# Cleared rows by ScalarE, pair sums in the last stage, a guard around unused positions, and products that nobody reads

## Chip, cores and metric

The kernel runs on one core of a Trainium2 chip. The metric is the device time of one execution in microseconds (us); the time before is the median of three runs. Engines are named as in the profile: PE is TensorE (PEld its weight loads), DVE is VectorE, ACT is ScalarE, POOL is GpSimd, SP is SyncE, whose queue issues most transfers.

## What is computed

An encoder layer over 1024 tokens of 1024 channels: a mixer (neighbourhood attention, RWKV-7 in both directions, pooling), a residual with layer norm, and then a mixture of experts. The change touches only the second half. There each token picks one of 4 groups and in it the best 2 of 8 experts; each expert is a gated MLP of width 512; the two results are weighted and added, and a second residual with layer norm ends the layer:

```
gate = pg_sel[:, None] * jax.nn.softmax(top_l, axis=-1)      # 2 weights for each token
hb = jax.nn.silu(xb @ w_gate[e]) * (xb @ w_up[e])            # for each block of an expert's tokens
y  = (hb @ w_down[e]) * wt[:, None]
f  = segment_sum(y, token)                                   # two rows for each token
x  = layer_norm(ALPHA * x + g2 * f) * ln2_gain + ln2_bias
```

## The kernel before

**Three stages matter.** The router (`route`, `router`) sorts tokens to experts; its instructions are ordered by a scheduler. The expert stage and the last stage (both in `experts`, the last one planned in `tail_plan`) are written out engine by engine, with semaphores.

**Router.** For each of the 2 x 8 columns of token places, GpSimd makes a one-hot matrix (L1267) and ScalarE scales it with the row number plus one (L1268). TensorE multiplies these with block one-hots (L1323), which gives for each of at most 50 positions the 128 rows that belong to it: `idx[:, g]` for reading, `idx[:, 50 + g]` for writing. An unused slot gets a row number beyond the last row, and the transfer skips it. So the buffers `xg` that receive rows must have been cleared: GpSimd does it with one memset of 4096 columns (L1275), behind its last one-hot (`issue_after`). A number for each position says how it is worked: 0 unused, 1 for 32 tokens, 2 for 64, 3 for 128. VectorE forms all these numbers in a chain of small operations (L1230 to L1356).

**Expert stage.** A position is up to 128 tokens of one expert. `pipeline` runs for TensorE, ScalarE and VectorE, `step(g)`: load the count of position g+1, `head(g)` (gate and up products, L1713 for 128 tokens, L1721 for fewer), `rows(g+1)` (transposes of the next position's rows, L1692), `down(g-1)` (down products, L1747 and L1758), `turn(g)` (transposes of the hidden values, L1728), then `step(g+1)`. TensorE is thus always one position ahead with heads. `by_size` chooses one of three bodies by branches; with few tokens the products write to 32 or 64 columns of the array (128\*32, 128\*64 in the profile) and several share it. The first 16 positions are always used; from there on branches ask whether a position is used (`if_used`). Steps are nested, so after the last used position, 36 here, TensorE and VectorE enter 37 with count 0, skip its bodies, do `down(36)` and jump to the end. GpSimd's queue gathers rows of a position from HBM (`gather`, L1648, size chosen by branches), four positions ahead, and scatters results to `ys` in HBM (L1656), to row 2 x token + j for choice j. SyncE's queue loads expert weights into three buffers (L1577); weights of the first three positions are loaded in the router. Those of position g wait for the gate-up products of g-3.

**End of the expert stage.** SyncE (`finish`) loads gain and bias of the last norm into the first half of `xg` (`late`), the residual rows x1 (L1589), and once all scatters have landed the result rows of `ys` in eight transfers of 1 MB, `l0` to `l7` (L1595). In transfer tt partition p gets both rows of token 128 tt + p.

**Last stage.** For each of 8 tiles of 128 tokens: TensorE multiplies the two result rows with diagonal matrices of the gates (`dg`, built by ScalarE and VectorE, L1906 and L1907), 4 products 128\*128 by 512 columns; in tiles 2 and 5 two more products with `alpha` add the residual (L1866). Tile tt uses the pair of banks tt mod 3. Otherwise VectorE adds the residual while it sums (L1878); for tiles 2 and 5 ScalarE sums (L1875). Then mean (L1883, VectorE), squares and root (L1895, L1897, ScalarE), reciprocal and a product (L1887, L1888, VectorE), normalising (L1901, ScalarE), times gain and plus bias (L1891, L1892, VectorE), and the output transfer (L1639). Each engine works its list in order and waits by the lists' counts. [...]

## Time and profile before

| | us |
|---|---|
| median of three runs (1575.29 to 1577.81) | 1575.91 |
| the profiled execution | 1565.44 |
| its span, first to last instruction | 1563.6 |
| router's last part, until the expert stage opens | to 947.7 |
| expert stage | 947.7 to 1508.5 |
| last stage | 1508.5 to 1563.6 |

Over the span TensorE is busy 87%, VectorE 50%, ScalarE 37%, GpSimd 24%; the mean granted clock of TensorE is 0.924.

How to read the rows below. A timeline row has the start and the length in us, the engine, the line of the kernel, the operation, out<-in, shapes and the number of merged instructions; in brackets stands the idle time just before and what ended it ("issue": nothing that the profile shows). Product shapes are rows\*columns of the array, then the output. [...] A group row has the count, then busy us and mean ns of one, then idle time before.

### The profile page before, as it was taken

What the parts mean: (1) busy time and instruction counts of PE and PEld (TensorE: products, weight loads), DVE (VectorE), ACT (ScalarE), POOL (GpSimd) and SP (SyncE); (2) the same over time, 40 slices, a digit from 0 to 9 for tenths busy, and PEclk for the clock granted to TensorE, in tenths of its full rate; (3) what the DMA queues carried; (4) which work ended last, traced back from release to release, by engine and by line L of the source; (5) the groups of instructions that cost most, each with busy time, mean ns of one, the idle gap of its engine ahead of it and who ended that gap; (6) DMA issues with size and microseconds to landing.
All of it is one profiled execution on the core that took longest, in us unless ns stands there. A gap on an engine that the chain in (4) does not pass through costs nothing. (4 is left out here: it accounts for less than half of the span.)

```text
span 1563.6 us, 24661 instructions
## 1 busy us (share of the span) xinstructions
PE 1367.4 (87%) x8190; PEld 923.9 (59%) x8190; DVE 778.7 (50%) x2002; ACT 571.8 (37%) x1182; POOL 380.4 (24%) x442
## 2 busy tenths in 40 slices
PE   5989999988869899999899745999999999899856
PEld 5778778766546677677788643444444444444422
DVE  6775886855883566565667972111111121211117
ACT  5663433414575667676544430000001000100006
POOL 3331232351337313700403331011101101111000
PEclk8999999996868899989999857999999999999968
DMA  9868899866422325315564475898878987998764
GB/s 259 223 200 303 284 318 327 298 211 186 145 64 69 93 72 150 88 35 150 187 262 162 167 275 208 338 351 324 330 291 341 380 324 306 362 369 349 262 248 193
DMA packets 163373, 371.49 MB, mean 238 GB/s; under 512 B 22880, under 2 KB 99009, under 8 KB 154227
## 3 DMA queue, kind: packets, MB, share of 16 engines
q1 hardware_dynamic: 155555, 350.59, 63.2%
q0 software_dynamic: 7632, 18.51, 3.7%
q8 instruction: 106, 1.74, 0.4%
q14 instruction: 80, 0.66, 0.1%
HBM read 365.47 MB, written 65.44 MB: 276 GB/s over the span
## 5 line engine op out<-in xcount | busy, mean ns | idle before, releaser
L1713 PE MATMUL m_pgu<-w,m_xT 128*128 128x512 f32 x448 | 197.0, 598 | 7.4 <-issue 7.2
L1713 PEld LDWEIGHTS m_pgu<-w,m_xT 128*128 128x128 f32 x448 | 84.7, 192 | 110.4 <-issue 110.3
L1656 POOL DMA_INDIRECT ys_s<-m_y,m_idx x37 | 35.0, 946 | 467.4 <-DVE m_y L1786 266.5
L197 PE MATMUL pg<-ul,w_h 128*128 128x512 f32 x320 | 128.2, 401 | 0.2 <-DVE ul L295 0.2
L196 PE MATMUL pg<-uh,w_h 128*128 128x512 f32 x320 | 126.7, 402 | 1.4 <-ACT uh L294 0.7
L198 PE MATMUL pg<-uh,w_l 128*128 128x512 f32 x320 | 126.8, 396 | 0.0
L1721 PE MATMUL m_pgu<-w,m_xT 128*32 128x256 f32 (+1 forms) x1312 | 108.0, 420 | 8.7 <-issue 8.3
L1747 PE MATMUL m_py<-w,m_hT 128*128 128x512 f32 x224 | 98.7, 594 | 9.6 <-issue 9.6
L1825 DVE TENSOR_TENSOR m_h<-m_sil,m_pgu 128x512 f32<-128x512 f32 x14 | 9.6, 688 | 192.4 <-PE m_pgu L1713 192.4
L1721 PEld LDWEIGHTS m_pgu<-w,m_xT 128*32 128x32 f32 (+1 forms) x1312 | 53.6, 116 | 54.5 <-issue 34.2
L210 DVE SCALAR_TENSOR_TENSOR acc<-wm,sc_c,acc 128x256 f32<-128x256 f32 x112 | 62.3, 557 | 27.8 <-DMA wm<-in_w_mod_dram 18.9
L1747 PEld LDWEIGHTS m_py<-w,m_hT 128*128 128x128 f32 x224 | 41.5, 190 | 57.1 <-issue 57.1
L1828 DVE TENSOR_TENSOR m_h<-m_sil,m_pgu 64x256 f32<-64x256 f32 (+1 forms) x23 | 10.8, 471 | 121.0 <-ACT m_sil L1796 121.0
L196 PEld LDWEIGHTS pg<-uh,w_h 128*128 128x128 f32 x320 | 60.6, 191 | 15.3 <-ACT uh L294 1.6
L197 PEld LDWEIGHTS pg<-ul,w_h 128*128 128x128 f32 x320 | 61.0, 191 | 14.1 <-issue 0.7
L198 PEld LDWEIGHTS pg<-uh,w_l 128*128 128x128 f32 x320 | 61.1, 191 | 13.3 <-issue 0.7
L945 DVE SCALAR_TENSOR_TENSOR sn<-s,fc,sf 64x64 f32<-64x64 f32 x168 | 47.5, 283 | 41.7 <-PE s L936 38.6
L756 PE MATMUL g<-zi,bk 64*128 64x128 f32 x384 | 54.2, 320 | 15.2 <-DMA bk<-bkd 9.3
L1758 PE MATMUL m_py<-w,m_hT 128*32 128x256 f32 (+1 forms) x656 | 56.6, 418 | 12.2 <-issue 12.2
L1781 DVE TENSOR_TENSOR m_y<-m_py,m_g 128x512 f32<-128x512 f32 x28 | 19.4, 692 | 88.0 <-PE m_py L1747 88.0
L756 PEld LDWEIGHTS g<-zi,bk 64*128 64x128 f32 x384 | 46.6, 219 | 28.0 <-issue 10.6
L1786 DVE TENSOR_TENSOR m_y<-m_py,m_g 32x256 f32<-32x256 f32 (+1 forms) x82 | 37.0, 451 | 52.3 <-PE m_py L1758 51.1
(523 smaller groups left out, 3017.8 us busy)
## 6 DMA issues: line engine op xcount, KB each, us to landing
w<-in_moe_w_gate_dram SPq DMA_DIRECT2D x37, 2048.0 KB, 8.4
w<-in_moe_w_up_dram SPq DMA_DIRECT2D x37, 2048.0 KB, 12.9
w<-in_moe_w_down_dram SPq DMA_DIRECT2D x37, 2048.0 KB, 15.9
wm<-in_w_mod_dram SPq DMA_DIRECT2D x128, 128.0 KB, 4.6
w<-in_w_in_dram SPq DMA_DIRECT2D x21, 512.0 KB, 6.7
hd<-h SPq DMA_DIRECT2D x18, 512.0 KB, 4.5
wm<-in_w_mod_dram SPq DMA_DIRECT2D x16, 512.0 KB, 6.3
w<-ys_s SPq DMA_DIRECT2D x8, 1024.0 KB, 13.0
```

Source lines behind the costliest of these rows:

```text
L196: mm(out, lh[0], rh[0], start=start, stop=False)
L197: mm(out, lh[0], rh[1], start=False, stop=False)
L198: mm(out, lh[1], rh[0], start=False, stop=stop)
L210: nc.vector.scalar_tensor_tensor(acc, wm, self.sc_c[:, k:k + 1], acc, op0=OP.mult, op1=OP.add)
L756: nc.tensor.matmul(pa[h][:, j], bk[hs, j], zr[hs, j], start=True, stop=True)
L945: nc.vector.scalar_tensor_tensor(sn[H[h], H[h]], p[H[h], 2, H[h]], fc[H[h]], sf[H[h], H[h]], op0=OP.mult, op1=OP.add)
L1656: e.indirect_dma_start(out=self.ys_d, out_offset=off(idx[0:t, NP + g:NP + g + 1]), in_=y[0:t, g % NY], in_offset=None, bounds_check=2 * S ...
L1713: i = mm(pgu[q], xT[:, k], w[:, k], start=k == 0, stop=k == 7)
L1721: i = mm(pgu[0][o:o + t, 0:n], xT[:, k, 0:t], w[:, k, c:c + n], start=k == 0, stop=k == 7)
L1747: i = mm(py[nh], hT[:, 128 * f:128 * f + 128], wd[b][:, f, 512 * nh:512 * nh + 512], start=f == 0, stop=f == 3)
L1758: i = mm(py[0][o:o + t, 0:n], hT[:, 64 * j + t * a:64 * j + t * a + t], wd[b][:, f, c:c + n], start=f == 0, stop=f == 3)
L1786: i = e.tensor_mul(y[0:t, g % NY, c], py[0][t * j:t * j + t, 0:n], g2[0:t, c])
```

## The change

Four edits.

1. **Clear** (L1275): the memset of `xg` on GpSimd becomes a copy with scale 0 on ScalarE, behind ScalarE's last scaled one-hot.
2. **Front of the expert stage.** The first four gathers fetch all 128 slots of a position without asking its size, ahead of the loads of the counts. TensorE first runs four products into `ph`, which nobody reads. VectorE adds neighbouring columns of the identity into `pair`: column m has ones in rows 2m and 2m+1. SyncE issues four small transfers that put the gates into `rowg`, in the order of result rows (partition 2t + j).
3. **Guard** (`step`): for TensorE and VectorE, `head` and the next position's `rows` stand in one branch, `turn` and the next step in another, with `down(g-1)` between them. The inner branch around `turn` goes.
4. **Last stage.** Transfer tt now brings rows in order: partition p gets rows p and 128 + p of the tile's 256. `dg` is `pair` times the gate of each row, 64 columns wide, so that a product sums the two rows of 64 tokens at once: 4 products 128\*64 for a tile, into the upper and lower 64 partitions in turn. For all tiles but the last the residual comes from two `alpha` products, which those of tiles 0 and 1 do ahead of the loaded rows, followed by five products into the idle bank `ph`. The sums wait for each half by itself and run on ScalarE, those of tile 7 on VectorE. Normalising becomes two passes on VectorE: (x less the mean) times gain, then times the reciprocal root plus bias.

TensorE at the opening of the expert stage, before (`m_pT` are the banks of transposed rows, `w_7635` the buffer of position 0's weights):

```order
L1987 UNCONDITIONAL_BRANCH
L1681 UNCONDITIONAL_BRANCH
L1499 TENSOR_LOAD m_code
L1499 ISA x2
L1692 MATMUL m_pT<-cst,m_xg 128x128 x8
L1499 TENSOR_LOAD m_code
L1499 ISA x2
L1512 COMPARE_AND_BRANCH
L1721 MATMUL m_pgu<-w_7635,m_xT 32x256 x32
```

and after:

```order
L2017 UNCONDITIONAL_BRANCH
L1701 UNCONDITIONAL_BRANCH
L1783 MATMUL m_ph<-cst 128x512 x4
L1502 TENSOR_LOAD m_code
L1502 ISA x2
L1712 MATMUL m_pT<-cst,m_xg 128x128 x8
L1502 TENSOR_LOAD m_code
L1502 ISA x2
L1515 COMPARE_AND_BRANCH
L1741 MATMUL m_pgu<-w_7635,m_xT 32x256 x32
```

The four products without a reader stand ahead of the first count's load and of the transposes, which wait for the gathered rows.

TensorE between the transposes of one position and the bodies of the next one's head, from position 17 on, before:

```order
L1733 COMPARE_AND_BRANCH
L1728 MATMUL m_ph<-cst,m_h 128x128 x2
L1733 UNCONDITIONAL_BRANCH
L1728 MATMUL m_ph<-cst,m_h 128x128 x2
L1524 UNCONDITIONAL_BRANCH
L1524 COMPARE_AND_BRANCH
L1499 TENSOR_LOAD m_code
L1499 ISA x2
L1512 COMPARE_AND_BRANCH
L1721 MATMUL m_pgu<-w,m_xT 32x256 x32
L1512 UNCONDITIONAL_BRANCH
```

and after:

```order
L1752 COMPARE_AND_BRANCH
L1748 MATMUL m_ph<-cst,m_h 128x128 x2
L1752 UNCONDITIONAL_BRANCH
L1748 MATMUL m_ph<-cst,m_h 128x128 x2
L1502 TENSOR_LOAD m_code
L1502 ISA x2
L1527 COMPARE_AND_BRANCH
L1515 COMPARE_AND_BRANCH
L1741 MATMUL m_pgu<-w,m_xT 32x256 x32
L1515 UNCONDITIONAL_BRANCH
```

The test for a used position now stands behind the count's load and skips the whole head with the next rows; the pair of branches ahead of the load is gone.

TensorE from the opening of the last stage on, before (`m_pgu`, `m_pT`, `m_py` are the three pairs of banks; products with `cst` are those with `alpha`):

```order
L1866 MATMUL m_pgu0<-w0_7635,m_xg 128x512 x2
L1866 MATMUL m_pgu1<-w0_7635,m_xg 128x512 x2
L1866 MATMUL m_pT0<-w0_7635,m_xg 128x512 x2
L1866 MATMUL m_pT1<-w0_7635,m_xg 128x512 x2
L1866 MATMUL m_py0<-w0_7635,m_xg 128x512 x2
L1866 MATMUL m_py0<-w2,cst 128x512
L1866 MATMUL m_py1<-w0_7635,m_xg 128x512 x2
L1866 MATMUL m_py1<-w2,cst 128x512
```

and after:

```order
L1886 MATMUL m_pgu0<-w2,cst 128x512
L1886 MATMUL m_pgu1<-w2,cst 128x512
L1886 MATMUL m_pT0<-w2,cst 128x512
L1886 MATMUL m_pT1<-w2,cst 128x512
L1940 MATMUL m_ph<-w2,cst 128x512 x5
L1893 MATMUL m_pgu0<-w0_7635,m_xg 64x512 x2
L1893 MATMUL m_pgu1<-w0_7635,m_xg 64x512 x2
L1893 MATMUL m_pT0<-w0_7635,m_xg 64x512 x2
L1893 MATMUL m_pT1<-w0_7635,m_xg 64x512 x2
L1886 MATMUL m_py0<-w2,cst 128x512
L1886 MATMUL m_py1<-w2,cst 128x512
L1893 MATMUL m_py0<-w0_7635,m_xg 64x512 x2
```

Residuals of tiles 0 and 1 and five unread products now stand ahead of the first product that needs loaded rows; from tile 2 on each tile's residual stands behind the products of the tile before.

The diff, cut to what the prediction speaks of:

```diff
         for j in range(16):
-            last = nc.gpsimd.tensor_scalar(ohr[:, j], C["iota128"], row[:, j:j + 1], None, op0=OP.is_equal)
-            nc.scalar.activation(ohs[:, j], ohr[:, j], AF.Copy, scale=C["orow1"][:, j:j + 1])
+            nc.gpsimd.tensor_scalar(ohr[:, j], C["iota128"], row[:, j:j + 1], None, op0=OP.is_equal)
+            last = nc.scalar.activation(ohs[:, j], ohr[:, j], AF.Copy, scale=C["orow1"][:, j:j + 1])
...
         with self.rtc.issue_after(last.ins):
-            nc.gpsimd.memset(self.xg, 0.0)
+            nc.scalar.activation(self.xg, C["iota128"][:, 0:1, None].to_broadcast([128, NX, D]), AF.Copy, scale=0.0)
...
             def step(g, old, c):
                 new = size(e, g + 1) if g + 1 < NP else None
-                head(g, c)
-                if new is not None:
-                    rows(g + 1, new)
-                if g and down:
-                    by_size(e, old, lambda t: down(g - 1, t))
...
+                if not down:
+                    first()
+                    rest()
                 else:
-                    if_used(e, new, g + 1, lambda: step(g + 1, c, new))
+                    if_used(e, c, g, first)
+                    if g:
+                        by_size(e, old, lambda t: down(g - 1, t))
+                    if_used(e, c, g, rest)
...
-                        e.dma_start(yall[tt], self.ys_d[256 * tt:256 * tt + 256, :].rearrange("(t j) n -> t j n", j=2)
+                        e.dma_start(yall[tt], self.ys_d[256 * tt:256 * tt + 256, :].rearrange("(s p) n -> p s n", s=2)
...
+                for s in range(2):
+                    for j in range(2):
+                        e.dma_start(rowg[j:128:2, s, :], self.gtw[64 * s:64 * s + 64, j, :]).then_inc(sem("rowg"), 16)
...
                 for g in range(NX):
+                    e.indirect_dma_start(
+                        out=xg[:, g], out_offset=None, in_=self.u2d, in_offset=off(idx[:, g:g + 1]),
+                        bounds_check=S - 1, oob_is_err=False).then_inc(sem(f"xg{g}"), 16)
+                for g in range(NX):
                     c.append(size(e, g))
-                    gather(g, c[g])
...
+                for _ in range(4):
+                    mm(ph, ident, self.cst[:, 0:512], start=True, stop=True)
...
+            for h in range(2):
+                for s in range(2):
+                    i = e.matmul(pf(tt)[h][64 * s:64 * s + 64, :], dg[:, 2 * tt + s], yall[tt][:, s, hs[h]],
+                                 start=not inside(tt), stop=True)
...
+            op("dve", "xm", tt, [("mean", tt), ("mm1", tt), ("late", 32)], lambda e: e.scalar_tensor_tensor(
+                xm(tt), of[tt], col(tt, 12), gain, op0=OP.add, op1=OP.mult))
...
+            op("dve", "add", tt, [("rec", tt), ("xm", tt), ("sq", tt)], lambda e: e.scalar_tensor_tensor(
+                of[tt], xm(tt), col(tt, 15), bias, op0=OP.mult, op1=OP.add))
...
+        op("pe", "idle", 0, [], lambda e: [e.matmul(idle, alpha, x1a[0][:, hs[0]], start=True, stop=True) for _ in range(5)][-1])
```

(The product loop is given in one piece; in the diff the loop over halves calls `half(e, h)`.)

## Rows read from the trace of the kernel before

**Rows 1.** Windows of the expert stage and the last stage: busy time of each engine.
```profile
947.70:1508.50 560.80, 509.74 (x3048) 252.78 (x3048) 93.92 (x187) 51.72 (x121) 70.98 (x74) 0.97 0.84 323
...
1508.50:1563.60 55.10, 33.79 (x72) 14.61 (x72) 31.59 (x72) 25.57 (x41) 0.01 (x1) 0.78 0.59 233
```

**Rows 2.** Timeline, the expert stage's first 15 us: SyncE's queue and TensorE.
```profile
947.66 0.33 SPq L1635 DMA_DIRECT2D m_g<-rows_s  x1
...
951.89 1.97 PE L1692 MATMUL m_pT<-cst,m_xg 128*128 128x128 f32 x8 [6.40 <-DMA m_xg<-u_s,m_idx]
...
954.33 5.69 PE L1721 MATMUL m_pgu<-w,m_xT 128*32 128x256 f32 x64 [0.47 <-DVE m_xT L1768]
...
960.40 0.36 SPq L1577 DMA_DIRECT2D w<-in_moe_w_gate_dram  x1
...
962.34 3.66 PE L1721 MATMUL m_pgu<-w,m_xT 128*32 128x256 f32 x64 [0.69 <-issue]
```

**Rows 3.** Timeline of the last stage: TensorE's tiles 0, 1 and 7, VectorE's end.
```profile
1516.35 6.32 PE L1866 MATMUL m_pgu<-w,m_xg 128*128 128x512 f32 x8 [11.04 <-DMA w<-ys_s]
...
1522.51 3.60 PE L1866 MATMUL m_pT<-w,m_xg 128*128 128x512 f32 x8
...
1546.54 3.60 PE L1866 MATMUL m_pT<-w,m_xg 128*128 128x512 f32 x8
...
1559.35 1.23 DVE L1892 TENSOR_TENSOR w<-w,m_xg 128x1024 f32<-128x1024 f32 x1
```

**Rows 4.** Groups of the last stage (columns as in the page's part 5).
```profile
L1892 DVE TENSOR_TENSOR w<-w,m_xg 128x1024 f32<-128x1024 f32 x8 | 9.8, 1224 | 0.3
...
L1901 ACT ACTIVATE w<-w,m_ls 128x1024 f32<-128x1024 f32 x8 | 9.9, 1240 | 4.6 <-DVE m_ls L1888 4.6
...
L1878 DVE SCALAR_TENSOR_TENSOR w<-w,m_pgu 128x512 f32<-128x512 f32 x6 | 3.9, 684 | 12.8 <-PE m_pgu L1866 12.8
```

**Rows 5.** Timeline of the router's end: GpSimd's clear and two operations on VectorE.
```profile
935.98 3.50 POOL L1275 MEMSET m_xg<- 128x4096 f32 x1
...
936.00 3.58 DVE L1312 TENSOR_SCALAR rt<-rt 128x16 int32<-128x16 int32 x1
...
939.59 0.18 DVE L1342 TENSOR_SCALAR m_code<-m_code 1x50 int32<-1x50 int32 x1
```

**Rows 6.** Windows of 1 us in which the granted clock (PEclk) changes.
```profile
958.00:959.00 1.00, 1.00 (x20) 0.52 (x16) 0.00 (x0) 0.00 (x0) 0.00 (x0) 0.75 0.07 29
...
1504.00:1505.00 1.00, 1.00 (x6) 0.17 (x2) 0.00 (x0) 0.00 (x0) 0.00 (x0) 0.69 0.00 0
...
1508.00:1509.00 1.00, 0.00 (x0) 0.00 (x0) 0.71 (x4) 0.00 (x0) 0.51 (x1) 0.52 0.03 8
...
1521.00:1522.00 1.00, 1.00 (x2) 0.32 (x2) 0.00 (x0) 0.00 (x0) 0.00 (x0) 0.66 0.99 418
```

**Rows 7.** End of the expert stage: one window, then timeline of three engines.
```profile
1484.00:1496.00 12.00, 7.43 (x60) 3.15 (x56) 2.35 (x5) 0.96 (x2) 0.86 (x1) 0.93 0.99 374
...
1497.03 2.44 ACT L1906 ACTIVATE m_xg<-cst,m_gt 128x128 f32<-128x128 f32 x8 [5.19 <-issue]
...
1498.76 6.55 PE L1758 MATMUL m_py<-w,m_hT 128*64 128x512 f32 x16 [7.33 <-issue]
...
1508.29 1.66 DVE L1907 TENSOR_SCALAR m_xg<-cst,m_gt 128x128 f32<-128x128 f32 x8 [1.55 <-issue]
```

**Rows 8.** Timeline: narrow products, and the same transposes behind wide and narrow ones.
```profile
1002.32 3.65 PE L1758 MATMUL m_py<-w,m_hT 128*64 128x512 f32 x16
...
1001.34 1.05 PE L1692 MATMUL m_pT<-cst,m_xg 128*128 128x128 f32 x8
...
1104.18 1.16 PE L1692 MATMUL m_pT<-cst,m_xg 128*128 128x128 f32 x8
```

**Rows 9.** Timeline of TensorE: an idle time inside transposes, and a head without one.
```profile
1478.27 0.33 PE L1728 MATMUL m_ph<-cst,m_h 128*128 128x128 f32 x1 [2.00 <-issue]
...
1403.03 13.97 PE L1713 MATMUL m_pgu<-w,m_xT 128*128 128x512 f32 x32
```

More of the change, by code (lines that the diff above doesn't have):

```diff
@@ L1840, in experts, with tail_plan @@
         ctx.close()
-    def tail_plan(self, sem, yall, x1a, of, ls, gain, bias, banks, junk):
+    def tail_plan(self, sem, yall, x1a, of, ls, gain, bias, pair, rowg, banks, idle, junk):
         lists = {"pe": [], "act": [], "dve": []}
@@ L1917, in tail_plan @@
                 mean(tt)
[L1918 to L1922 removed]
+                centre(tt)
             if tt:
                 normal(tt - 1)
[L1925 to L1926 removed]
+        for tt in range(8):
+            if inside(tt):
+                sums(tt)
+            deviation(tt)
         def at(name, tt):
```

99 lines of the change are left out of this document (49 added, 50 removed).

## Prediction

> **What bounds the kernel now.** I read the windows by stage first, then the order of time at the three places that the change touches, then the groups of the last stage. In the expert stage TensorE is busy 509.74 of 560.80 us and the DMA engines 0.84 of the time [rows 1]: both are near their limit and take turns, so an edit inside buys little, but a stage that begins earlier ends earlier by as much, since weights and products start off the same first result (SyncE issues the next expert's weights at 960.40, when position 0's gate-up products end [rows 2]). The last stage is another matter: in 55.10 us no engine is busy more than 33.79 [rows 1]. TensorE waits 11.04 us for its rows, starts at half clock [rows 3], and from then on the tiles march at VectorE's pace. The reader is to see there that VectorE has per tile two sums of 0.68 and two passes of 1.22 over 1024 columns [rows 4]: with the small ones about 4.0 us, for eight tiles 32 us, which ends at 1560.6 [rows 3]; 3.0 us of output transfer follow to the span's 1563.6.
>
> The profiled execution took 1565.44 us, 1.8 more than its span. The median of the timed runs, 1575.91, is 10.5 us above it, which no row explains; I take the gain in us from the profile off that median.
>
> **The change part by part.**
>
> *Clearing on ScalarE.* GpSimd's clear runs from 935.98 for 3.50 us; a VectorE operation on 16 columns that begins at 936.00, the last of four that stand alike, ends only at 939.58, while the next one takes 0.18 [rows 5]. VectorE stood still as long as GpSimd wrote. These operations lead to the row lists and so to the stage's end. With the clear on ScalarE they should take about 0.2: 939.59 less 936.2 is **3.4 us**. ScalarE's clear starts behind its last one-hot, which follows GpSimd's last; GpSimd's own clear stood right behind that, so ScalarE's begins 0.5 us after it, at 936.5. 4096 columns at 1.24 us per 1024 [rows 4] make 5.0 us at most, to 941.5; the stage, 3.4 us earlier, closes at 944.2 (947.66 now [rows 2]), so 2.7 us cover it. Bounds: 3.5 if GpSimd's whole clear goes; 1.1 if ScalarE's took 10, twice my figure.
>
> *First rows and four products nobody reads.* The stage opens at 947.66 (call it B); TensorE's first transposes wait for rows until 951.89, B + 4.2; they take 1.97, the first gate-up 5.69, both mostly at half clock, and end at B + 12.35 [rows 2]. Now TensorE begins at B with four wide products, eight instructions of 0.43 us at full clock (56 of them between 1522.51 and 1546.54 [rows 3]), 0.86 at half. The clock was granted 6.6 us after work began at 951.89, 5.9 after 1498.76 and 5.3 after 1516.35 (a slice's mean of 0.75 puts the rise in its middle) [rows 2, 3, 6, 7]. So the eight end between B + 6.1 and B + 6.8, 2 us and more behind the rows, which they also cover: the unconditional gathers, the row swaps of the gates on SyncE's queue and the extra addition on VectorE cost nothing while they last. Behind them the transposes take 1.05 [rows 8], the copy 0.5, the gate-up 3.66, as position 1's does, instead of 5.69 [rows 2]: B + 11.3 to 12.0. **0.7 us** gained; bounds 1.5 gained, and 1.0 lost if the clock comes late and the eight take 7 us or if a fetch delays them.
>
> *The guard.* Position 37 is the only unused one that is entered. TensorE passes it skipping two gate-up bodies, then the transposes, then one down-projection, before the last products: 7.33 us of issue time up to 1498.76. ScalarE, with one far jump in the same stretch, needed 5.19, to 1497.03; both stood while the x1 rows filled the DMA engines (0.99 to 1496) [rows 7]. One jump over the whole head instead of three should bring TensorE to where ScalarE was: **1.7 us**, all on the path to the last scatter. Bounds: 0; and 6 if the jump costs nothing.
> [...]
>
> *The last stage.* Per tile, TensorE now has a wide residual, two products or 4 instructions (4 x 0.43 = 1.72), and four narrow ones, 8 instructions. Narrow ones exist: 16 of 128*64 take 3.65 [rows 8], 0.228 each, half of a wide one, since two go side by side into the two halves of the columns. 8 x 0.228 = 1.83. Two changes of shape per tile: the same eight transposes take 1.05 behind wide products and 1.16 behind narrow ones [rows 8], 0.11 each, 0.22. Sum 3.77 us per tile.
> VectorE keeps a mean (0.2), one pass of centring and gain, a reciprocal (0.16) and one pass with the bias: 2 x 1.22 + 0.4 = 2.85 [rows 4]. ScalarE takes two sums (half of 1.24 each), a square (1.24), and for read-outs, root and the round trip to VectorE an estimated 0.7: 3.2 [rows 4]. So TensorE sets the pace. The rows of tile 0 come at 1516.35, those of tile 1, 1 MB later, at 1519.2 if they run at the 374 GB/s of the x1 rows [rows 7]. Residuals 0 and 1 and five unread products (18 instructions, 7.7 us) fill the wait, if TensorE's jump into this stage is like VectorE's (1.55 [rows 7]): from 1506.9, before the clock fell in 1508 [rows 6], to 1514.6. Tile 0's products end at 1518.3, tile 1's at 1521.1, tiles 2 to 6 at 3.77 each at 1540.0. Then ScalarE's sums and VectorE's mean (1.3), the centring of 6 and end of 5 (2.85), the sums of 7 (1.34), mean and centring (1.4), the ends of 6 and 7 (2.8): 1549.6, against 1560.6. **11.0 us.** Bounds: 12.6 with no price for the shapes; 8 if the unread products push tile 0 to 1520. The 4 KB pieces of the new loads cost nothing: the x1 rows, read in such pieces, kept the engines at 0.99 [rows 7].
>
> Sum: 3.4 + 0.7 + 1.7 + 11.0 = 16.8. 1565.44 becomes 1548.6, the median 1575.91 becomes **1559.1**.
>
> **The rivals.**
> *Serial narrow products.* If the pairs, whose weights both differ (in the rows read they share them), do not overlap, a product costs 8 x 0.43 = 3.43 and a tile 5.15 + 0.2: the last product ends at 1553, the last addition at 1559, and 2 us remain: 1575.91 - 7.8 = 1568. For it: the weights; against: the 0.228.
> *A long pause at each change of shape.* If TensorE stood still for a whole wide instruction, 0.43, at each change, a tile would pay 0.86 instead of 0.22; five tiles of the path lose 3.2: 1562. Against it stands the 0.11.
> [...]
> *The unread products stand in the way.* The clock falls before TensorE gets to the residuals, 18 instructions then take 10.5 us, tile 0 starts at 1519 to 1521, and at the front the eight end at B + 7: 1.9 to 3.9 lost in the last stage and 1.2 in front: 1563. For it: the clock fell 2.7 us after the last product (in 1508 [rows 6]), and the jump time of 1.55 is VectorE's.
> *The start is swallowed.* Weights, not products, set the expert stage and their transfers gain nothing from B: only the 13 us of the end stay, 1563.
> *Slower: code that comes late.* From position 16 the guard moves TensorE's branch behind the next count's load and gives VectorE one more per position, and so shifts where code breaks off; 21 such positions are passed. In one place TensorE stood still 2.00 us between two transposes that wait for nothing [rows 9]. If each position cost 1.0 more, the stage would be 21 us longer: 1575.9 - 16.8 + 21 = 1580. It decides from 16.8 / 21 = 0.80 us each. Against it: with a branch pair in the same place today, the gate-up at 1403.03 starts without idle time [rows 9].
>
> **How the numbers follow.** The forecast 0.71, with 1553 to 1564 of its own (from a gain of 23, the upper bounds without the free jump's full 6, to one of 12, where two terms fall to their lower ones); serial products 0.06; long pauses 0.04; unread products in the way 0.09; start swallowed 0.03; late code 0.07, of which 0.04 slower and 0.03 near the time before. The range takes in all but the late code and some of the forecast's lower edge: 1552 to 1568. A measurement can tell 0.2% here, 3.2 us: faster 0.93, within 0.03, slower 0.04.
>
> **What would show it.** In the profile after: no VectorE operation of 3.5 us near 936 and a stage that opens 3.4 us earlier; eight wide instructions before the first transposes and a first gate-up near 3.7 us; less than 6 us of issue before the last down products; in the last stage 1.8 us for eight narrow instructions, tiles 3.8 us apart, VectorE idle between them, and 33 us from the first product on loaded rows to the last addition, 44 now. Wrong it would be made by narrow instructions 0.43 apart, a clock of 0.50 while tile 0 runs, or new idle time before heads from position 16 on.

## The result, and the profile after

The changed kernel takes 1558.26 us (median of 15 runs, 1550.21 to 1568.29), the kernel before on the same chip 1575.64 (15 runs, 1564.68 to 1579.61): a ratio of 0.990 with a 95% interval of 0.988 to 0.992, or 17.4 us gained (12.6 to 18.9 by the interval). The forecast was 1559.1, faster, in a range of 1552 to 1568. The forecast held; of its four terms two were right in size and cause, one was right in sign for a partly wrong reason, and one fell.

The profiled execution took 1559.82 us, its span is 1557.6, only 6.0 less than the span before. Where the rest went is told below: the middle of the expert stage, which the change hardly touches, took 12 us longer in this execution. The pieces on either side of it can be compared one by one.

The router's end, in the timeline: ScalarE's clear, the VectorE operation that stood still in [rows 5], and the first product of the row lists.

```profile
935.00 3.60 ACT L1275 ACTIVATE m_xg<-cst 128x4096 f32<-128x4096 f32 x1
...
934.62 0.15 DVE L1312 TENSOR_SCALAR rt<-rt 128x16 int32<-128x16 int32 x1
...
937.08 3.58 PE L1323 MATMUL pg<-rt,rt 128*128 128x50 f32 x16 [3.52 <-DVE rt L1320]
```

L1312 takes 0.15 us instead of 3.58. Counted from the end of ScalarE's last one-hot (which stands at the same point of both programs), the products of the row lists begin 1.99 us later instead of 5.45, and the expert stage opens 7.74 us later instead of 11.20: 3.46 us gained. The clear itself took 3.60 us and is over 4 us before the stage opens at 942.83.

The start of the expert stage, which answers to [rows 2]: SyncE's queue and TensorE.

```profile
942.83 0.33 SPq L1648 DMA_DIRECT2D m_g<-rows_s  x1
...
942.88 6.06 PE L1783 MATMUL m_ph<-cst 128*128 128x512 f32 x8 [2.22 <-PEq L2017]
...
948.78 1.05 PE L1712 MATMUL m_pT<-cst,m_xg 128*128 128x128 f32 x8
...
950.31 3.66 PE L1741 MATMUL m_pgu<-w,m_xT 128*32 128x256 f32 x64 [0.48 <-DVE m_xT L1789]
...
954.35 0.36 SPq L1590 DMA_DIRECT2D w<-in_moe_w_gate_dram  x1
```

The four products that nobody reads (x8 in the row: each shows as two instructions) end 6.1 us after the opening, the first gate-up products at 953.97, 11.14 us after it (12.36 before): 1.22 us gained. SyncE issues the next weights at once, as before.

The end of the expert stage, which answers to [rows 7], and the first products of the last stage, in the timeline of ScalarE and TensorE.

```profile
1502.54 2.02 ACT L1934 ACTIVATE m_xg<-m_pair,m_rowg 128x64 f32<-128x64 f32 x8 [4.54 <-issue]
...
1504.61 5.06 PE L1776 MATMUL m_py<-w,m_hT 128*64 128x512 f32 x16 [7.02 <-issue]
...
1509.61 1.98 PE L1886 MATMUL m_pgu<-w,cst 128*128 128x512 f32 x4
```

TensorE still stands for 7.02 us ahead of the last down products, 7.33 before. Behind them it goes on without idle time.

The last stage, which answers to [rows 3]: TensorE's unread products, tiles 0 and 1, the residuals of tiles 3 and 4 (the step from tile to tile), tile 7, and VectorE's last pass. Then two groups of VectorE, which answer to [rows 4], and the windows of the two stages, as in [rows 1]. A window row has, there as here, the stretch, its length, then busy time and instructions of PE, PEld, DVE, ACT and POOL, the granted clock as a share of full speed, the busy share of the DMA engines and GB/s.

```profile
1513.14 4.46 PE L1940 MATMUL m_ph<-w,cst 128*128 128x512 f32 x10
...
1520.78 3.36 PE L1893 MATMUL m_pgu<-w,m_xg 128*64 128x512 f32 x8 [3.18 <-DMA w<-ys_s]
...
1523.87 2.26 PE L1893 MATMUL m_pT<-w,m_xg 128*64 128x512 f32 x8
...
1529.84 1.98 PE L1886 MATMUL m_pgu<-w,cst 128*128 128x512 f32 x4
...
1533.62 1.98 PE L1886 MATMUL m_pT<-w,cst 128*128 128x512 f32 x4
...
1544.87 1.89 PE L1893 MATMUL m_pT<-w,m_xg 128*64 128x512 f32 x8
...
1553.29 1.28 DVE L1923 SCALAR_TENSOR_TENSOR w<-w,m_ls,m_xg 128x1024 f32<-128x1024 f32 x1
```

```profile
L1918 DVE SCALAR_TENSOR_TENSOR w<-w,m_ls,m_xg 128x1024 f32<-128x1024 f32 x8 | 10.3, 1285 | 0.3
L1923 DVE SCALAR_TENSOR_TENSOR w<-w,m_ls,m_xg 128x1024 f32<-128x1024 f32 x8 | 10.3, 1285 | 0.3
```

```profile
942.83:1512.87 570.04, 524.02 (x3064) 256.10 (x3065) 93.96 (x187) 51.35 (x121) 71.22 (x74) 0.96 0.82 318
1512.87:1557.60 44.73, 30.70 (x96) 9.82 (x94) 25.45 (x44) 22.30 (x53) 0.00 (x0) 0.90 0.73 288
```

From the first product on loaded rows (1520.78) to the end of the last addition (1554.57) pass 33.8 us, 44.2 before. From the end of the last down products to the end of the span pass 47.9 us, 58.3 before: 10.4 us gained. The tiles are 3.78 us apart. The five unread products end at 1517.6, 3.2 us ahead of the loaded rows, and the clock falls just as tile 0 begins, as this 1-us window shows (granted clock 0.57, third number from the end):

```profile
1521.00:1522.00 1.00, 1.00 (x4) 0.30 (x2) 0.00 (x0) 0.00 (x0) 0.00 (x0) 0.57 1.03 422
```

The four pieces (clear, start, wait before the last down products, last stage) give 3.46 + 1.22 + 0.31 + 10.36 = 15.4 us, inside the interval of what the medians gained, 12.6 to 18.9.

### The profile page after: what moved, and what is told of

It is laid out like the page before. It is cut to its first block, busy times and chain, and to the rows that moved or that the text cites. A ratio compares the mean times of both kernels' runs of the same rounds, so it can differ in the third digit from the quotient of the medians.

```text
span 1557.6 us, 24746 instructions
## 1 busy us (share of the span) xinstructions
PE 1377.9 (88%) x8228; PEld 922.7 (59%) x8228; DVE 769.1 (49%) x1975; ACT 571.5 (37%) x1195; POOL 377.4 (24%) x441
## 5 line engine op out<-in xcount | busy, mean ns | idle before, releaser
L196 PEld LDWEIGHTS pg<-uh,w_h 128*128 128x128 f32 x320 | 60.2, 190 | 15.4 <-ACT uh L294 1.9
L945 DVE SCALAR_TENSOR_TENSOR sn<-s,fc,sf 64x64 f32<-64x64 f32 x168 | 47.6, 283 | 41.8 <-PE s L936 38.7
L756 PEld LDWEIGHTS g<-zi,bk 64*128 64x128 f32 x384 | 46.5, 218 | 28.2 <-issue 11.3
L1807 DVE TENSOR_TENSOR m_y<-m_py,m_g 32x256 f32<-32x256 f32 (+1 forms) x82 | 37.0, 451 | 49.0 <-PE m_py L1776 47.8
## 6 DMA issues: line engine op xcount, KB each, us to landing
w<-in_moe_w_up_dram SPq DMA_DIRECT2D x37, 2048.0 KB, 12.7
```

What stands on the lines that cost most here:

```text
L196: mm(out, lh[0], rh[0], start=start, stop=False)
L756: nc.tensor.matmul(pa[h][:, j], bk[hs, j], zr[hs, j], start=True, stop=True)
L945: nc.vector.scalar_tensor_tensor(sn[H[h], H[h]], p[H[h], 2, H[h]], fc[H[h]], sf[H[h], H[h]], op0=OP.mult, op1=OP.add)
L1807: i = e.tensor_mul(y[0:t, g % NY, c], py[0][t * j:t * j + t, 0:n], g2[0:t, c])
```

## Experiments

Each kernel is the changed one with the edit shown. The ratios are to the kernel before, timed beside it on the same chip. The profile of each is one execution; "end" in the last column is the end of the span.

| kernel | median us | ratio, 95% interval | opening to end of first gate-up, us | wait before the last down products, us | last down products to end, us |
|---|---|---|---|---|---|
| before | 1575.64 | | 12.36 | 7.33 | 58.3 |
| changed | 1558.26 | 0.990 [0.988, 0.992] | 11.14 | 7.02 | 47.9 |
| no_tail | 1568.28 | 0.9945 [0.992, 0.997] | 11.79 | 7.04 | 58.4 |
| no_guard | 1555.93 | 0.989 [0.986, 0.993] | 11.08 | 6.83 | 48.2 |
| no_clear | 1564.76 | 0.993 [0.990, 0.995] | 11.01 | 6.79 | 48.3 |
| no_unread | 1564.77 | 0.993 [0.991, 0.995] | 10.97 | 6.57 | 48.4 |
| after_again | 1561.08 | 0.990 [0.986, 0.994] | 11.37 | 7.10 | 47.3 |
| x1b_late | 1559.16 | 0.990 [0.986, 0.994] | 10.86 | 4.36 | 47.3 |
| more_unread | 1553.32 | 0.985 [0.982, 0.988] | 11.23 | 5.58 | 47.1 |
| better2 | 1556.76 | 0.988 [0.985, 0.992] | 10.84 | 4.27 | 47.8 |
| front0 | 1564.49 | 0.992 [0.988, 0.995] | 12.01 | 6.97 | 47.2 |
| front_old | 1562.56 | 0.991 [0.988, 0.994] | 12.29 | 6.80 | 47.0 |
| jumps3 | 1562.01 | 0.991 [0.988, 0.994] | 11.15 | 4.30 | 47.0 |
| better1 | 1559.46 | 0.988 [0.984, 0.991] | 10.93 | 4.06 | 47.6 |

The times of single executions of one kernel spread over 9 to 20 us, so effects of 1 to 3 us are read from the pieces in the profiles and not from the medians.

### The last stage undone (no_tail)

```diff
-        tail = self.tail_plan(sem, yall, x1a, of, ls, gain, bias, pair, rowg, ...)
+        tail = self.tail_plan(sem, yall, x1a, of, ls, gain, bias, ...)    # tail_plan of before
-                        ... self.ys_d[256 * tt:256 * tt + 256, :].rearrange("(s p) n -> p s n", s=2)
+                        ... self.ys_d[256 * tt:256 * tt + 256, :].rearrange("(t j) n -> t j n", j=2)
```

> The changed kernel with the last stage of the kernel before (its loads, diagonal matrices, products, sums and passes); the other three edits stay. Theory (each part acts where it stands, and the last stage carries most): the prediction gave the last stage 11.0 us and the trace of the changed kernel reads 10.4 (47.9 us from the end of the last down products to the span's end, 58.3 before), so the median of the changed kernel, 1558.3, becomes 1568.7 to 1569.3, a ratio to the kernel before of 0.9955, and the stretch from the last down products to the end is again 58.3. Rival (the expert stage itself became quicker position by position, since the guard took out a pair of branches, and the last stage gives less in the median than in one profile): 1562 to 1565, ratio 0.992 or 0.993.

In its timeline tile 0, whose first instructions and wait stand here, and VectorE's last pass:

```profile
1525.08 6.22 PE L1888 MATMUL m_pgu<-w,m_xg 128*128 128x512 f32 x8 [11.14 <-DMA w<-ys_s]
...
1567.99 1.22 DVE L1914 TENSOR_TENSOR w<-w,m_xg 128x1024 f32<-128x1024 f32 x1
```

The stage is the old one to a tenth: 44.1 us from tile 0 to the last addition, 58.4 from the last down products to the end. So the 10.4 us belong to the last stage alone. The median, 1568.28 at 0.9945, lies between theory (0.9955) and rival (0.992 to 0.993), and its interval, 0.9921 to 0.9969, holds the theory and nearly all of the rival; the trace decides for the theory, and leaves open whether the other edits bring a few us more than their pieces show.

### The clear undone (no_clear)

```diff
-            nc.gpsimd.tensor_scalar(ohr[:, j], ...)
-            last = nc.scalar.activation(ohs[:, j], ...)
+            last = nc.gpsimd.tensor_scalar(ohr[:, j], ...)
+            nc.scalar.activation(ohs[:, j], ...)
...
-            nc.scalar.activation(self.xg, C["iota128"][:, 0:1, None].to_broadcast([128, NX, D]), AF.Copy, scale=0.0)
+            nc.gpsimd.memset(self.xg, 0.0)
```

> The changed kernel with the clear of the row buffers as GpSimd's memset again. Theory (VectorE stands still while GpSimd writes, and the row lists wait for it): a VectorE operation on 16 columns near the memset takes some 3.5 us again, and from the last one-hot of ScalarE to the first product of the row lists pass 5.4 us (5.45 before, 1.99 after); median 3.4 us longer, 1561.7. Rival (the stage that opens earlier only waits longer for weights or rows): the stall is there, but the median stays within 1 us of 1558.3.

The timeline has the stall again, on the same operation:

```profile
942.87 3.50 POOL L1275 MEMSET m_xg<- 128x4096 f32 x1
942.90 3.58 DVE L1312 TENSOR_SCALAR rt<-rt 128x16 int32<-128x16 int32 x1
...
946.48 0.18 DVE L1342 TENSOR_SCALAR m_code<-m_code 1x50 int32<-1x50 int32 x1
```

From the last one-hot to the row lists' products 5.43 us, to the opening of the expert stage 11.19: against 1.98 to 2.00 and 7.73 to 7.75 in the twelve profiles with ScalarE's clear, so 3.45 us. The ratio, 0.993 against 0.990, agrees with 3.4 us, with intervals that overlap.

### The guard undone (no_guard)

```diff
-                    if_used(e, c, g, first)
-                    if g:
-                        by_size(e, old, lambda t: down(g - 1, t))
-                    if_used(e, c, g, rest)
+                head(g, c)
+                if new is not None:
+                    rows(g + 1, new)
+                if g and down:
+                    by_size(e, old, lambda t: down(g - 1, t))
...
+                    if_used(e, c, g, lambda: step(g + 1, c, new))
```

> The changed kernel with the step of the kernel before: the test for a used position stands between positions again, and TensorE passes position 37 with three jumps. Theory A (the wait before the last down products, 7.33 us before and 7.02 after, ends some 3 us after the last x1 rows have landed, whatever the number of jumps): wait 7.0 to 7.5, median 0.3 us longer, 1558.6. Theory B (the prediction's: each jump costs, and 7.02 is an unlucky execution): wait near 8.7, median 1.7 us longer, 1560.0. Theory C (the guard costs or gains time at each of the 21 positions from 16 on): the median moves by 4 us or more either way.

TensorE's last down products in its timeline:

```profile
1500.68 5.19 PE L1768 MATMUL m_py<-w,m_hT 128*64 128x512 f32 x16 [6.83 <-issue]
```

Three jumps instead of one, and the wait is 6.83, not 8.7. Theory B falls, and with it the prediction's third term. The ratio, 0.989 with an interval of 0.986 to 0.993, gives no sign of C, but is too wide to exclude 4 us. Theory A gives the right wait; whether its cause is right, the next kernel asks.

### Code behind the x1 rows (x1b_late, jumps3)

```diff
                     for i, w in enumerate((wg[2], wu[2])):
+                        if i:
+                            e.wait_ge(*tail.at("dg0", 7))
                         e.dma_start(w.rearrange("p (t k) n -> p t (k n)", k=2), self.x1d[512 * i:512 * i + 512, :] ...)
```

> The changed kernel, in which SyncE issues the second half of the x1 rows (2 MB, used from tile 4 on) only when ScalarE has made its last diagonal matrix, behind its own jump into the last stage. The first half then lands by 1493, 4 us before TensorE's far jump begins. Theory A (TensorE's wait before the last down products is a fetch of code that queues behind the x1 rows; in the six profiles so far it is 6.6 to 7.3 us with one jump or three and ends some 3 us after those rows have landed): wait 2 to 4 us instead of 7.0, ScalarE's 1.5 to 3 instead of 4.5, the median 3 to 5 us shorter, 1553 to 1555. Theory B (the far jump itself costs 7 us): wait 6.5 to 7.3, median unchanged or longer by what the late rows cost.

The issue of the x1 rows, now 15.49 us from the first to the second, and TensorE's last down products, in the timeline; then a window of 1 us inside TensorE's wait, and two later ones:

```profile
1478.04 15.49 SPq L1604 DMA_DIRECT2D w<-x_s  x2
...
1492.78 6.35 PE L1778 MATMUL m_py<-w,m_hT 128*64 128x512 f32 x16 [4.36 <-issue]
```

```profile
1490.00:1491.00 1.00, 0.00 (x0) 0.00 (x0) 0.00 (x0) 0.00 (x0) 0.55 (x1) 1.00 0.00 0
...
1493.00:1494.00 1.00, 1.00 (x4) 0.35 (x4) 0.00 (x0) 0.13 (x1) 0.00 (x0) 0.50 0.12 16
...
1498.00:1499.00 1.00, 1.00 (x6) 0.20 (x2) 0.00 (x0) 0.00 (x0) 0.00 (x0) 0.88 1.02 418
```

The wait falls from 7.02 to 4.36 us, and ScalarE's from 4.54 to 2.28. In four profiles with the late half TensorE waits 4.06 to 4.36 and ScalarE 2.24 to 2.34; in the ten others 5.58 to 7.33 and 3.18 to 5.97. So 2.7 us of the 7.0 hang on the x1 rows: theory A is right in cause, but not in size (it had 2 to 4 us of wait, and a median 3 to 5 us shorter).

That the wait is a fetch of code shows in the trace's transfers, which name the queues that bring instructions. The queue q8 in the transfer view, number of packets and MB first, for 1489.30 to 1490.60 of this kernel and for 1501.10 to 1502.50 of the changed one:

```profile
q8 instruction: 1, 0.02, 5.6%
```

```profile
q8 instruction: 1, 0.02, 5.5%
```

In all fourteen profiles just one such packet, of 16 KB, lands inside TensorE's wait. With the late half it starts 0.9 to 1.1 us into the wait, in the ten others 2.1 to 3.8 us into it, and in each profile the wait ends 2.2 to 2.4 us after the packet has landed (x1b_late: landed after 2.13 us, wait 4.36; changed kernel: 4.81 and 7.02). What fills the last 2.2 us is not shown. The x1 rows thus delay the fetch; the 4.3 us that are left pass with transfer engines that are idle most of the time (0.00 in 1490).

The gain is not kept whole: the clock is at half speed when the down products start and until 1498.2, and they take 6.35 us instead of 5.06 (6.35 to 6.59 in the four with the late half; 5.06 to 6.61, mean 5.69, in the ten others). From the start of the last gate-up products to the end of these down products the four kernels read 21.8 to 23.1 us (mean 22.3), the ten others 23.3 to 25.1 (mean 24.2): 1.9 us, too little for the medians to show (1559.16 against 1561.08 for the changed kernel timed beside it).

What the jumps cost when no transfer stands in the way is the question to the same kernel with the step of before, without products at the front and with nine unread ones in the last stage.

> The late second half of the x1 rows with the step of the kernel before (three jumps over position 37 instead of one), no products at the front, nine unread ones in the last stage. With the guard and the late half TensorE's wait before the last down products was 4.36 and 4.27 us. Theory A (a fetch takes its time, and jumps past code that is already on the chip cost little): 4.2 to 4.8. Theory B (the prediction's: each further jump costs some 0.8 us once no transfer stands in the way): 5.5 to 6.5.

```profile
1508.77 6.59 PE L1770 MATMUL m_py<-w,m_hT 128*64 128x512 f32 x16 [4.30 <-issue]
```

4.30 with three jumps, 4.06 to 4.36 with one: theory A. The number of jumps costs nothing that these profiles can tell, behind busy transfer engines (6.83 and 7.33 us with three, 5.58 to 7.10 with one) or idle ones. One packet of q8 lands inside each wait, and three jumps instead of one bring no second one.

### The unread products (no_unread, more_unread, front0, front_old)

```diff
-                for _ in range(4):
-                    mm(ph, ident, self.cst[:, 0:512], start=True, stop=True)
...
-        op("pe", "idle", 0, [], lambda e: [e.matmul(idle, alpha, ...) for _ in range(5)][-1])
```

> The changed kernel without the products that nobody reads, four at the front of the expert stage and five in the last stage; everything else stays. Front, theory A (they raise the clock while the rows come): the first transposes take 1.97 and the first gate-up products 5.69 again and end 12.0 to 12.4 us after the stage opens (11.1 with the products). Front, theory B (the gain came from the unconditional gathers): they end at 11.1 to 11.5 also without. Last stage, theory A (five end 3.2 us before tile 0, the clock falls anyway as tile 0 begins, 0.57 in that us, so that they buy little): tiles 0 and 1 take 3.7 and 2.5 to 3.5 us (3.36 and 2.26 with them), 0.5 to 1.5 lost. Theory B (the prediction's, that they keep tile 0 at the full clock): 3 us lost. Median 1560 by both A.

The front of this kernel in the timeline, then the 1-us window in which its clock rises:

```profile
943.30 0.33 SPq L1648 DMA_DIRECT2D m_g<-rows_s  x1
...
947.53 1.97 PE L1712 MATMUL m_pT<-cst,m_xg 128*128 128x128 f32 x8 [6.40 <-DMA m_xg<-u_s,m_idx]
...
949.98 4.29 PE L1741 MATMUL m_pgu<-w,m_xT 128*32 128x256 f32 x64 [0.48 <-DVE m_xT L1787]
```

```profile
951.00:952.00 1.00, 1.00 (x24) 0.57 (x19) 0.00 (x0) 0.00 (x0) 0.00 (x0) 0.84 0.88 324
```

The transposes begin 4.23 us after the opening and take 1.97, just as in [rows 2], but the gate-up products take 4.29 and not 5.69, since the clock rises 3.8 us after work began, not 6.6: they end at 10.97 without any unread product. That left two readings, told apart by two more kernels. The first leaves out the four at the front alone (and has nine in the last stage).

> The changed kernel without the four products at the front of the expert stage, and with nine unread products in the last stage. So far the first gate-up products ended 12.36 us after the stage opened in the kernel before, 10.79 to 11.79 (mean 11.14) in eight profiles with the four products, and 10.97 in the one profile without them, in which the clock rose 3.6 us after the first transposes began (6.4 in the kernel before). Theory A (the moment at which the clock rises after work begins varies from one execution to the next by 2 to 3 us, and 10.97 was an early one): 11.5 to 12.5. Theory B (the four products bring nothing, the gain is the gathers'): 10.8 to 11.2 again. Last stage: tile 0 in 1.94 us, from its first product to the last addition 32.8, as with nine before.

The second also gathers as before:

```diff
                 for g in range(NX):
-                    e.indirect_dma_start(out=xg[:, g], ...).then_inc(sem(f"xg{g}"), 16)
-                for g in range(NX):
                     c.append(size(e, g))
+                    gather(g, c[g])
                 step(0, c)
```

> As the one without the four products at the front, and with the first gathers as in the kernel before, each behind the load of its count and with its size. This is the old front, except for the gates' four transfers and the extra addition. Theory A (the rows come 4.23 us after the opening with either kind of gather, and only the clock's rise differs): the first transposes begin 4.2 us after the opening, the gate-up products end at 11.0 to 12.5. Theory B (the unconditional gathers make the stage's start quicker): the transposes begin at 4.2 but position 1's rows come later, the gate-up products end at 12.3 or later.

The gate-up products of both, in their timelines:

```profile
953.03 5.40 PE L1741 MATMUL m_pgu<-w,m_xT 128*32 128x256 f32 x64 [0.47 <-issue]
```

```profile
950.85 5.57 PE L1738 MATMUL m_pgu<-w,m_xT 128*32 128x256 f32 x64 [0.47 <-DVE m_xT L1784]
```

They end 12.01 and 12.29 us after the opening. A fourth kernel without the four products, jumps3, reads 11.15. So theory A holds, though 12.29 lies at the edge of theory B's 12.3: the rows come 4.2 to 4.3 us after the opening with either kind of gather, and what differs is when the clock rises. It rises 3.8, 4.1, 6.0, 6.4 and 6.6 us after work began in no_unread, jumps3, front0, front_old and the kernel before, and the ends stand in the same order: 10.97, 11.15, 12.01, 12.29 and 12.36. With the four products the nine profiles read 10.84 to 11.79, mean 11.14; without them, with the new gathers, 10.97, 11.15 and 12.01, mean 11.38; with the old front 12.29 and 12.36. The two of the old front lie above all others, but with so few executions and a spread of 1 us the share of each edit stays open; the four products alone are worth 0.2 us by these means (0.6 against all five starts without them), not shown to differ from nothing.

The times say something else, and the pieces do not explain it. The four kernels without the four products read 0.991 to 0.993, the seven that keep them together with the clear and the new last stage 0.985 to 0.990: some 5 us by the means. front0 and more_unread differ by these products alone (timed on different chips) and read 0.992 [0.988, 0.995] and 0.985 [0.982, 0.988]. If the products are worth that much, it would have to lie in the middle of the expert stage, which takes 530.4 to 532.6 us in the four and 521.4 to 532.4 in the seven; but it took 519.9 in the kernel before, without such products. The cause is not shown.

In the last stage no_unread took 3.68 and 2.22 us for tiles 0 and 1 (3.36 and 2.26 with the five): 34.1 us from tile 0 to the last addition instead of 33.8. In these two executions five products bought 0.3 us, less than the 0.5 to 1.5 of theory A; two other profiles with five read 32.9, 1.2 less than without. The median, 1564.77 at 0.993, lies some 3 us above what both pieces explain, with an interval that overlaps the changed kernel's. This kernel has nine:

```diff
-        op("pe", "idle", 0, [], lambda e: [e.matmul(idle, alpha, ...) for _ in range(5)][-1])
+        op("pe", "idle", 0, [], lambda e: [e.matmul(idle, alpha, ...) for _ in range(9)][-1])
```

> The changed kernel with nine unread products in the last stage instead of five (18 instructions, 7.7 us at full clock). In the trace of the changed kernel five end at 1517.6, 3.2 us before the rows of tile 0, and the clock falls to 0.57 just in the us in which tile 0 begins. Theory A (the idle time made the clock fall): the nine end at 1521.0, 0.2 us behind the rows, tile 0 takes 1.9 us instead of 3.36 and tile 1 1.9 instead of 2.26, TensorE's last product ends 1.5 us sooner after the last down products, and the median falls by 1 to 1.5 us. Theory B (they take more from tile 0 than the clock gives, or the loads set the pace): last product no sooner, median 0 to 1 us longer.

TensorE's unread products and tile 0, then VectorE's last pass:

```profile
1511.43 7.89 PE L1940 MATMUL m_ph<-w,cst 128*128 128x512 f32 x18
...
1519.25 1.94 PE L1893 MATMUL m_pgu<-w,m_xg 128*64 128x512 f32 x8
...
1550.74 1.28 DVE L1923 SCALAR_TENSOR_TENSOR w<-w,m_ls,m_xg 128x1024 f32<-128x1024 f32 x1
```

Tile 0 takes 1.94 us, and 32.8 pass to the end of the last addition: 1.0 us less than in the first profile of the changed kernel, the lower end of theory A's 1 to 1.5. TensorE's last product ends 0.84 us sooner behind the last down products, where theory A had 1.5. With nine all six profiles have tile 0 at 1.94. With five it varies, as the second profile of the changed kernel and that of x1b_late show.

> The changed kernel itself, as a mark on this chip for the others of this call, and a second profile of its expert stage. From the opening of the expert stage to the end of the last down products its first profile took 566.8 us, that of the kernel before 557.6, although the products at the front end 1.2 us sooner. Theory A (executions differ by this much, whatever the kernel): this profile differs by several us from 566.8, and the median stays at 0.99 of before. Theory B (the guard or the front makes the stage longer): again 565 to 568.

```profile
1524.56 1.94 PE L1893 MATMUL m_pgu<-w,m_xg 128*64 128x512 f32 x8 [3.33 <-DMA w<-ys_s]
```

Here the idle time is even longer (3.33 us, 3.18 in the first profile), and tile 0 runs at full clock: 32.9 us to the last addition instead of 33.8. The more_unread median, 1553.32 at 0.985, is lower than 1.0 us explains; its interval overlaps that of after_again, and the rest is not claimed.

### How long the expert stage takes (after_again and all others)

From the end of the first gate-up products to the transfer of the last norm's gain the program is the same in all fourteen profiles but for the guard. The windows of this stretch in the kernel before, the changed one and x1b_late:

```profile
960.02:1479.92 519.90, 484.30 (x2892) 241.74 (x2892) 89.20 (x176) 46.60 (x108) 65.27 (x68) 0.99 0.87 335
```

```profile
953.97:1485.75 531.78, 493.32 (x2892) 242.67 (x2893) 89.12 (x176) 46.61 (x108) 65.31 (x68) 0.97 0.84 328
```

```profile
955.77:1477.16 521.39, 488.28 (x2893) 241.37 (x2893) 89.11 (x176) 46.77 (x108) 65.44 (x68) 0.98 0.86 334
```

The same 2892 instructions (2893 in one record), and lengths from 519.9 to 531.8 us with a granted clock from 0.99 to 0.97. From the kernel before to the changed one TensorE is busy 9.0 us longer and idle 2.9 us longer. The clock stands at half speed for 6.8 us of this stretch in the kernel before, for 29.5 in the changed one and for 17.1 in x1b_late. Over the fourteen profiles, the four with less than 20 us at half speed read 519.9 to 524.6 us, the ten with 23.9 to 31.1 read 523.2 to 532.6: most of the spread goes with the clock. The eleven profiles with the guard read 521.2 to 532.6 (mean 528.6), the three without it 519.9, 524.6 and 530.5 (mean 525.0). By the measure of its expectation, from the opening to the end of the last down products, the second profile of the changed kernel reads 565.8 us, inside theory B's 565 to 568 and 1.1 from the first. Theory B falls all the same: no_clear and x1b_late have the guard and the front, and read 521.2 and 521.4 in this stretch. The 12 us between the two first profiles lie within the spread of executions. A cost or gain of the guard of some 3 us is neither shown nor excluded by so few.

### Two versions that go on (better1, better2)

Both have the late second half of x1 and nine unread products; better2 also this:

```diff
-        inside = lambda tt: tt < 7
+        inside = lambda tt: tt not in (4, 7)
```

> The changed kernel with the late second half of x1 and nine unread products in the last stage, all residuals of tiles 0 to 6 on TensorE. Wait before the last down products 4.2 to 4.5 us, tile 0 in 1.94 us, from its first product to the last addition 32.8. In the two profiles with the late half the shorter wait left the clock low for more of the last down products (6.35 us instead of 5.06), so that from the transfer of the last norm's gain to the end of these products they read 23.5 and 23.7 us, 23.9 in the changed kernel. Theory A (the clock takes back what the fetch gives): 23.5 to 23.8 again, median 1 us below the changed kernel's. Theory B: 22.5, median 2 to 4 us below, 1557 to 1559 where the kernel before takes 1576.

> Late second half of x1, nine unread products, and the residual of tile 4 added by VectorE instead of TensorE (four instructions and two changes of shape less on TensorE, two sums of 0.68 us more on VectorE, which has 0.4 to 0.9 us idle in each tile from 5 on; ScalarE loses two sums). Theory A for the first two: 3 to 5 and 1 to 1.5 us. For the third, theory A (TensorE sets the pace from tile 5 on): TensorE's last product 2.0 us sooner, last addition 1 to 2 us sooner; theory B (VectorE has no room: behind the sums of tile 4 it runs without idle time to the end): 0. Median by A 1550 to 1553, with theory B for the third 1552 to 1555.

better1 reads 4.06 us of wait, 21.8 from the start of the last gate-up products to the end of the last down products (the changed kernel 23.9), tile 0 at 1.94, and 1559.46 us, 0.988. From the transfer of the last norm's gain, the measure of its expectation, it reads 21.6: theory B or better. (By this measure x1b_late reads 22.0 and better2 23.5; the 23.7 of the expectation fits neither.) better2 takes 1556.76 us, 0.988, above both forecasts for it (1550 to 1553 and 1552 to 1555). In better2 TensorE's last product and VectorE's last pass are:

```profile
1534.25 1.89 PE L1895 MATMUL m_pT<-w,m_xg 128*64 128x512 f32 x8
...
1544.17 1.28 DVE L1925 SCALAR_TENSOR_TENSOR w<-w,m_ls,m_xg 128x1024 f32<-128x1024 f32 x1
```

The last product ends 23.1 us after tile 0's first instead of 25.0, but the last addition at 32.4 instead of 32.8: nearly theory B. From the mean of tile 6 at 1536.9 on VectorE works without a pause to 1545.5, and what TensorE gives there it can't use. Neither version is shown by the times to beat the changed kernel; by the pieces better1 has some 2 to 3 us less.

## Why the prediction was right, and where not

**What bounds.** The reading that the middle of the expert stage gives little and that the last stage is where the time lies held: 10.4 of the 15.4 us found in pieces. The choice to take the gain off the median, 10.5 us above the profile, also held: the middle of the expert stage in the profiled execution before was the shortest of fourteen (519.9 us), and whoever compares the two first profiles alone finds 6 us gained and not 17. That the median came within 0.9 us of the forecast is in part luck: the guard's missing 1.4 us and the last stage's 0.6 are made up by 0.5 at the start and by some 2 us that no piece holds. One reading of the kernel before was too simple. Eight tiles at 4.0 us from VectorE's first sum at 1522.71 would end at 1554.7 and not at 1560.6; VectorE stood idle in the first tiles, up to 2.92 us at a time, for values from ScalarE, while TensorE worked from 1516.35 to 1550.1 without idle time. The sum of the forecast does not use this reading.

**Clear, 3.4 us.** Right in size and cause: 3.46. VectorE no longer stands still. ScalarE's 4096 columns took 3.60 us where 5.0 were allowed, so the cover of 2.7 us was not needed. The length is in the rows: L1312 took 3.58 us beside GpSimd's memset of 3.50; with the clear on ScalarE it takes 0.15, and the one long operation beside that clear (L1320, 800 columns) 0.99, as before. By these rows an operation need not begin behind the memset to stand still: one of the four (L1340, 3.79 us, 0.33 in the changed kernel) begins 0.24 us ahead of the memset's row.

**Start, 0.7 us.** Measured 1.22; the end at 11.14 us lies just below the 11.3 to 12.0 forecast. The steps came as told (6.1 us of unread products, 1.05, 3.66). The failed step is the comparison: the 5.69 us before was one execution in which the clock rose late, and the same rows without unread products gave 4.29, 4.44 and 5.40. With the unread products TensorE turns to the transposes 5.4 to 6.6 us after the opening, while the rows come at 4.2; so an early rise of the clock without them ends as soon (10.97), and a late one some 1.2 us later (12.29). What the four products bring in the mean is not shown.

**Guard, 1.7 us.** Wrong: 0.3 in the wait, which stays at 7.02 us where less than 6 was to show. The failed step is "one jump over the whole head instead of three should bring TensorE to where ScalarE was". With the old step the wait is 6.83, with the late rows 4.30 for three jumps and 4.06 to 4.36 for one; in all of them the wait ends 2.2 to 2.4 us after one fetch of 16 KB has landed. The prediction saw that both engines stood while the x1 rows filled the DMA engines, and still priced the jumps, not the transfer. The lower bound, 0, was the right end. The upper one, 6 us for a jump that costs nothing, shows in no run: it would leave 1.33 of the 7.33 us, and the shortest wait is 4.06, in better1. The rival of late code from position 16, 1.0 us each, did not come: with the guard the middle of the expert stage takes 521.2 to 532.6 us, at most 12.7 more than before and not 21.

**Last stage, 11.0 us.** Measured 10.4. The tile was 3.78 us for 3.77 forecast: narrow instructions side by side take 0.24 us each, and neither serial pairs (3.43 for eight) nor a long pause at a change of shape appeared. The tile's step leaves some 0.1 us for a change of shape (3.78 less 4 x 0.43 and 8 x 0.228, for two of them), as the transposes of [rows 8] did. Two sizes were off. VectorE's passes take 1.28 us, not 1.22. And the rival of unread products in the way came with the opposite sign: TensorE needed no jump time of 1.55 us into this stage, so that the five ended 3.2 us ahead of the rows, and in this execution the clock fell as tile 0 began; that cost 0.85 us (33.8 against 32.9). A clock of 0.50 while tile 0 runs was named as a sign that the prediction is wrong; it came, at this small price. Another sign failed: VectorE was to be idle between the tiles, but from tile 1 to tile 4 it worked without a pause at 3.07 us a tile (2.85 forecast), and waited only before tiles 5 and 6 (0.62 and 0.85 us).

## What to carry to other kernels

Cut a change into pieces that begin and end at instructions which both programs have, and compare those: here single executions differ by 12 us in code that nobody touched, while the pieces repeat within 0.02 us (clear) to 1.8 us (the wait). An engine that stands with "issue" ahead of a far jump may be waiting for code behind a large transfer (here 2.7 of 7.0 us went with 2 MB of rows issued later); look at the queues that bring instructions, and move the transfer before you count the jumps. Products that nobody reads help most surely if they last until the rows are there: from tile 0 to the last addition pass 34.1 us without them (one profile), 32.9 to 33.8 with five (five profiles), 32.7 to 32.9 with nine (five).

## What the runs showed of the hardware

- TensorE's wait at a far jump, or at three, took 4.06 to 4.36 us with transfer engines that were mostly idle (in x1b_late 0.00 to 0.19 busy from 1488 to 1492) and 5.58 to 7.33 behind 4 MB of rows (in the changed kernel 1.05 and 1.01 busy in 1498 and 1499); ScalarE's took 2.24 to 2.34 and 3.18 to 5.97. In all fourteen profiles one 16 KB packet of an instruction queue lands inside TensorE's wait, which ends 2.2 to 2.4 us later.
- Shortening an idle time of TensorE gave back less than it saved: with 4.36 us of wait instead of 7.02 the clock stayed low for more of the following products, and these took 6.35 us instead of 5.06; in the means 2.5 us less of wait left 1.9.
- After idle time of 3.2 to 3.5 us the clock sometimes had fallen when work began again (tile 0 in 3.36 to 3.55 us in three profiles) and sometimes not (1.94 in two, with 3.33 and 3.36 us of idle time). After the opening of the expert stage it rose 3.7 to 6.6 us after work began (fourteen profiles).
- In one and the same stretch of the expert stage the clock stood at half speed for 6.8 to 31.1 us, and the stretch took 519.9 to 532.6.
- Eight narrow instructions (128\*64 by 512 columns), in pairs with two different weights, take 1.94 us, eight wide ones 3.60.
